# Three pairs in the seven products of SwiGLU's last down projection, and the norm's squares added on GpSimd

## The chip, the cores and the metric

The kernel runs on one core of a Trainium2 chip. The metric is the device time of one execution in microseconds (us). TensorE (PE in the profile) multiplies matrices, VectorE (DVE) and ScalarE (ACT) do elementwise work, GpSimd (POOL) does elementwise work and issues some DMAs, SyncE (SP) issues the other DMAs. A matmul result lands in a bank of PSUM; everything else lives in SBUF.

## What is computed

A trunk of two layers over a prompt of 512 tokens and a sample of 256, all in fp32. Each layer has a SwiGLU, a mixer (two kinds) and a second SwiGLU; a norm stands ahead of each and at the end.

```python
def swiglu(h, wg, wu, wd):
    return (jax.nn.silu(h @ wg) * (h @ wu)) @ wd      # 1024 -> 2816 -> 1024
def rmsnorm(x, g):
    return x * lax.rsqrt(jnp.mean(x * x, axis=-1, keepdims=True) + EPS) * g
def even_layer(x, ...):
    x = x + 0.5 * swiglu(rmsnorm(x, f1_n), f1_g, f1_u, f1_d)
    x = x + mixer_ab(rmsnorm(x, mix_n), ...)
    x = x + 0.5 * swiglu(rmsnorm(x, f2_n), f2_g, f2_u, f2_d)
def odd_layer(x, ...):      # the same with mixer_c, neighbourhood attention
```

## The kernel before, in words

The 768 tokens are the free dimension, in two halves of 384 (`HALVES`); the 1024 channels of x are eight tiles `x[0..7]` of 128 partitions. Each fp32 product is made of three single-pass matmuls by `mm3`: operands are split into a high part and the rest, and hi*hi, lo*hi and hi*lo are summed in PSUM. A weight tile of 128x512 is split by `wsplit`: ScalarE casts `whi`, VectorE subtracts for `wlo` (both in rings of five tiles, so that splits can run some way ahead of TensorE).

A SwiGLU goes by 11 pairs of 256 hidden channels (`NPAIR`). Its down projection is worked off for two pairs at a time by a 2x2 scheme of seven products in place of eight (Strassen and Winograd): the products are named by their data operand, b11, b21, t1, t2, t3, n4 and b22, and need sums of weight blocks (`sums`: s1 to s4, on VectorE or by accumulating DMAs) and of data blocks (`combine`). `down_last` does the last pairs and adds to x. Before, it takes pairs 8 and 9 through the seven products, 24 matmuls each, and pair 10 as a plain product (`plain`), 96 matmuls, with its own split weights (`lasts`) and operands (`operand`). The four calls are: layer 0's first SwiGLU, followed by the first mixer ("m0"); its second, followed by a SwiGLU ("f"); layer 1's first, followed by the second mixer ("m1"); its second, followed by the final norm ("last"). In "f" and "last" the order of the products is such that half 0 is done well ahead of half 1 (`lag`).

When a tile of x has its last addition, `final` calls `norm_add`: ScalarE squares it (`sq`), and VectorE adds the square to `acc` (L281). Once all eight tiles of a half are in, TensorE multiplies `ones` with `acc` (a sum over channels), ScalarE moves it to a small tile `sm`, GpSimd raises it to the power -1/2 (`sm<-sm,minus`, L321), and TensorE transposes the result (`ident,sm`). Ahead of a mixer, `final` also multiplies x by the gain and splits it (`xh` on ScalarE L992, `xl` on VectorE L993). The second mixer begins on GpSimd with ten additions of a mask `mb` and a bias (`add<-mb,ba` and `add<-mb,bb`, L1531); `mb` is cast in two pieces by VectorE from a loaded tile `mf`, whose buffer the second load shares.

TensorE's order is written by hand, by the order in which the code issues matmuls and by delays for the norms (`DELAY0`, `DELAYM` and others); the orders of the other engines come from a scheduler.

## Time and profile before

| what | value |
|---|---|
| median of three runs | 2553.0 us (2552.46 to 2553.01) |
| the profiled execution's own time | 2551.25 us |
| its span, from the first to the last instruction | 2549.5 us |
| mean granted TensorE clock | 0.999 |
| TensorE busy | 2532.9 us |
| VectorE busy | 2092.9 us |
| ScalarE busy | 1368.9 us |
| GpSimd busy | 323.5 us |

All times of single instructions are from that one execution. In lists of instructions the columns are start, duration, engine, line, operation, output<-inputs, shapes, and "xN" for N in a row; a bracket at the end gives the idle time of the engine before it and what ended it. Groups give busy time and mean nanoseconds. Rows of waits read: who waited for whom, us in total, times, longest.

### The profile page before, as it was taken

The numbers are of one execution on the slowest core, as the hardware profiler recorded it, in microseconds if no ns is written. First come the engines' busy times: TensorE is split into PE (matmuls) and PEld (weight loads), VectorE is DVE, ScalarE is ACT, GpSimd is POOL, SyncE is SP. The second block draws the span as 40 slices with busy tenths as digits, with TensorE's granted clock in tenths as the row PEclk, the third lists the DMA queues.
The fourth block names the chain that finished last, engine by engine and source line by source line (L and its number), as shares of the span: only waits on it lengthen the run. The fifth ranks groups of instructions, "written<-read, shape, count | busy, mean of one in ns | idle before, by whom it ended". The sixth has DMA issues, their size and how long they took to land.

```text
span 2549.5 us, 42554 instructions
## 1 busy us (share of the span) xinstructions
PE 2532.9 (99%) x15160; PEld 2459.3 (96%) x15160; DVE 2092.9 (82%) x4199; ACT 1368.9 (54%) x2843; POOL 323.5 (13%) x398
## 2 busy tenths in 40 slices
PE   9999999999999999999999999999999999999998
PEld 9999999988899999999999999998999899999998
DVE  8987888888879778888988888886667598878887
ACT  7544455546665545445655445554555475444553
POOL 1110111000111111110111011102112111101100
PEclk9999999999999999999999999999999999999999
DMA  8654555432256455552665455432222256545441
GB/s 238 159 133 119 132 134 147 146 94 64 77 142 175 117 128 127 131 130 80 156 150 135 119 128 125 120 127 69 65 61 78 76 150 166 131 121 125 124 125 53
DMA packets 187156, 310.88 MB, mean 122 GB/s; under 512 B 31680, under 2 KB 46528, under 8 KB 186944
## 3 DMA queue, kind: packets, MB, share of 16 engines
q1 hardware_dynamic: 149248, 240.49, 29.5%
q0 software_dynamic: 36864, 67.13, 16.9%
q8 instruction: 119, 1.95, 0.3%
q14 instruction: 93, 0.76, 0.1%
q10 hardware_dynamic: 832, 0.55, 0.1%
HBM read 298.65 MB, written 15.07 MB: 123 GB/s over the span
## 4 chain that ended last, share of the span: by engine, by line
PE 92%; DVE 4%; ACT 1%; issue 1%; DMA 1%; POOL 0%; ACTq 0%; DVEq 0%; SPq 0%; POOLq 0%
PE ps_mm L191 60%; PE ps_aux L191 30%; PE ps_aux L202 1%; DVE wlo L168 1%; DMA x<-in_x 0%; DMA s<-in_w 0%; DMA raw<-in_w 0%; DVE u L587 0%; DVE s L745 0%; DVE tl L255 0%; ACT p L1209 0%; ACT whi L167 0%; ACT ug L1484 0%; DVE o L1393 0%; DVE db L255 0%
## 5 line engine op out<-in xcount | busy, mean ns | idle before, releaser
L167 ACT CAST whi<-s 128x512 fp32r<-128x512 f32 x508 | 310.6, 621 | 384.5 <-PE ps_mm L191 199.0
L168 DVE TENSOR_TENSOR wlo<-s,whi 128x512 fp32r<-128x512 f32 x508 | 345.0, 687 | 173.6 <-ACT whi L167 152.1
L148 POOL DMA_DIRECT2D s<-in_w x256 | 224.0, 912 | 1440.0 <-DVE db L255 376.2
L167 ACT CAST whi<-rawp 128x512 fp32r<-128x512 f32 x344 | 211.5, 619 | 255.1 <-issue 100.0
L168 DVE TENSOR_TENSOR wlo<-rawp,whi 128x512 fp32r<-128x512 f32 x344 | 234.1, 685 | 23.2 <-ACT whi L167 14.2
L191 PE MATMUL ps_mm<-db,whi 128*128 128x384 f32 (+1 forms) x948 | 240.2, 334 | 0.0
L191 PE MATMUL ps_aux<-dt,whi 128*128 128x384 f32 x880 | 223.3, 334 | 0.0
L191 PEld LDWEIGHTS ps_mm<-db,whi 128*128 128x128 f32 x948 | 170.8, 188 | 0.0
L191 PE MATMUL ps_mm<-db,wlo 128*128 128x384 f32 (+1 forms) x474 | 158.3, 334 | 0.8 <-DVE wlo L168 0.8
L191 PEld LDWEIGHTS ps_aux<-dt,whi 128*128 128x128 f32 x880 | 158.9, 188 | 0.0
L191 PE MATMUL ps_aux<-dt,wlo 128*128 128x384 f32 x440 | 147.2, 335 | 0.4 <-DVE wlo L168 0.3
L167 ACT CAST whi<-raw 128x512 fp32r<-128x512 f32 x164 | 100.3, 619 | 68.6 <-PE ps_mm L191 44.6
L168 DVE TENSOR_TENSOR wlo<-raw,whi 128x512 fp32r<-128x512 f32 x146 | 98.9, 686 | 21.3 <-ACT whi L167 20.4
L587 DVE TENSOR_TENSOR u<-ps_aux,u 128x384 f32<-128x384 f32 x176 | 97.1, 552 | 7.7 <-PE ps_aux L191 7.7
L1209 ACT ACTIVATE p<-p,st 128x256 f32<-128x256 f32 (+3 forms) x144 | 69.1, 481 | 50.5 <-DVE st L1204 50.4
L191 PEld LDWEIGHTS ps_mm<-db,wlo 128*128 128x128 f32 x474 | 89.0, 188 | 1.4 <-DVE wlo L168 1.4
L581 ACT COPY u<-ps_mm 128x384 f32<-128x384 f32 x176 | 83.4, 474 | 1.9 <-PE ps_mm L191 1.6
L191 PEld LDWEIGHTS ps_aux<-dt,wlo 128*128 128x128 f32 x440 | 82.6, 188 | 1.0 <-DVE wlo L168 1.0
L745 DVE TENSOR_TENSOR s<-s,rawp 128x512 f32<-128x512 f32 x120 | 81.9, 687 | 2.0
L597 ACT ACTIVATE u<-u 128x384 f32<-128x384 f32 x88 | 46.2, 525 | 67.2 <-DVE u L596 67.1
L745 DVE TENSOR_TENSOR s<-rawp,s 128x512 f32<-128x512 f32 x120 | 81.9, 682 | 0.1
L191 PE MATMUL ps_aux<-dn,whi 128*128 128x384 f32 x320 | 81.2, 334 | 0.0
(772 smaller groups left out, 8228.7 us busy)
## 6 DMA issues: line engine op xcount, KB each, us to landing
rawp<-in_w SPq DMA_DIRECT2D x384, 256.0 KB, 3.2
s<-in_w SPq DMA_DIRECT2D x256, 256.0 KB, 2.8
s<-in_w POOLq DMA_DIRECT2D x256, 256.0 KB, 4.9
raw<-in_w SPq DMA_DIRECT2D x163, 256.0 KB, 2.9
xdm<-x SPq DMA_DIRECT2D x16, 384.0 KB, 2.3
x<-in_x SPq DMA_DIRECT2D x16, 192.0 KB, 4.6
x<-xdm SPq DMA_DIRECT2D x8, 384.0 KB, 4.9
tab<-skew SPq DMA_DIRECT2D x8, 256.0 KB, 4.0
```

What stands on the lines that cost most here:

```text
L148: self.nc.gpsimd.dma_start(f, y, accum_op=ALU.add)
L167: i = nc.scalar.copy(hi, src).ins
L168: self.behind = i, (eng or nc.gpsimd).tensor_tensor(out=lo, in0=src, in1=hi.bitcast(F32), op=ALU.subtract).ins
L191: self.nc.tensor.matmul(out, lhsT=lhsT, rhs=rhs, start=start, stop=stop, **kw)
L202: self.nc.tensor.transpose(out, src, self.ident)
L581: nc.scalar.copy(e[n, out], bank[key, n])
L587: nc.vector.tensor_tensor(out=t, in0=bank[key, n], in1=t, op=ALU.add)
L597: nc.scalar.activation(t, t, AF.Silu, scale=-1.0 if i else 1.0)
L745: f = lambda o, x, y: self.nc.vector.tensor_tensor(out=o, in0=x, in1=y, op=ALU.add)
L1209: nc.scalar.activation(outs[i - n0], outs[i - n0], AF.Exp, scale=-1.0, bias=mn[:, i : i + 1], accum_out=sm[:, i : i + 1])
```

## The change

`down_last` takes all three last pairs through the seven products, 36 matmuls each. A product works off pair 8 for its four banks, then pairs 9 and 10 bank by bank, so that banks are finished one after the other; the product that finishes half 1 in "f" (b22) and the last one in "m0" and "m1" (n4) take all three pairs bank by bank (`once`), and in "last" `ending` does the same with the narrow column slices. The code for the plain pair goes (`plain`, `lasts`, `operand`, `quads`, and `wsplit`'s kept and negated forms). In the three downs that are not followed by the end, `norm_add` puts the addition of squares on GpSimd (`aside`), and `final` calls `norm_add` after the gain and split of x, not ahead of them.

```diff
-            self.summed = i, nc.vector.tensor_tensor(out=self.acc[:, a:b], in0=self.acc[:, a:b], in1=sq, op=ALU.add).ins
+            eng = nc.gpsimd if self.aside else nc.vector
+            self.summed = i, eng.tensor_tensor(out=self.acc[:, a:b], in0=self.acc[:, a:b], in1=sq, op=ALU.add).ins
...
-        self.down_last(pre, range(NPAIR - 3, NPAIR - 1), d, hs[NPAIR - 1])
+        self.down_last(pre, range(NPAIR - 3, NPAIR), d, operands(NPAIR - 1))
...
-            t = s[n, "s2"] = self.fw.tile([P, 4, P], F32, tag="s", name=name, bufs=8)
+            t = s[n, "s2"] = a11 if n == NPAIR - 1 else self.fw.tile([P, 4, P], F32, tag="s", name=name, bufs=8)
...
+        def part(st, p, b, key, j, start, cols=slice(0, H)):
+            self.mm3(
+                bank[key, j][:, cols], (st[0][:, j, :], st[1][:, j, :]), [t[:, cols] for t in d[p][b]],
+                start and p == pairs[0], p == pairs[-1], not start,
+            )
+
+        def product(w, b, key, start, then, once=False):
+            for ps in (pairs,) if once else (pairs[:1], pairs[1:]):
+                st = {p: self.wsplit(w[p], nc.vector) for p in ps}
+                for j in range(4):
+                    for p in ps:
+                        if start and p == pairs[0]:
+                            bank[key, j] = self.psum()[:, :H]
+                        part(st[p], p, b, key, j, start)
+                    if ps[-1] == pairs[-1]:
+                        then(j)
...
+        def seed(j):
+            bank["Y", j] = self.psum(self.aux, "aux")[:, :H]
+            nc.scalar.copy(bank["Y", j], bank["X", j])
+
+        def below(j):
+            out(4 + j, 0, "Y")
             if not lag:
+                self.final(4 + j, H, T)
+
+        def ending():
+            st = {p: self.wsplit(s4[p], nc.vector) for p in pairs}
+            for js, cuts in ((0, 1), ((0, H),)), ((2, 3), CUTS):
                 for a, b in cuts:
                     for j in js:
+                        for p in pairs:
+                            part(st[p], p, "b22", "Z", j, False, slice(a, b))
+                        out(j, 1, "Z", a, b, j == 3)
                     if cuts is CUTS:
                         self.spawn(self.finish(1, H + a, H + b))
 
+        self.aside = not ends
+        more(own, 4)
+        product(w["a11"], "b11", "X", True, seed)
+        more(own, 2)
+        s2 = sums("s2")
+        product(w["a12"], "b21", "X", False, lambda j: out(j, 0, "X"))
+        more(self.later, 3)
+        product(s2, "t2", "Y", False, lambda j: add(j, 1, bank["Y", j]))
+        more(own, 5)
+        s4 = sums("s4")
+        fifth = sums("s1"), "t1", "Z", True, lambda j: add(4 + j, 1, bank["Z", j])
+        seventh = sums("s3"), "t3", "Y", False, lambda j: add(4 + j, 1, bank["Y", j])
+        third = s4, "b22", "Z", False, lambda j: out(j, 1, "Z")
+        fourth = w["a22"], "n4", "Y", False, lambda j: out(4 + j, 0, "Y")
         if lag:
+            product(*seventh)
+            product(*fourth)
             self.half_done(0)
+            product(*fifth[:4], lambda j: out(4 + j, 1, "Z"))
+            if ends:
+                ending()
+            else:
+                product(*third, True)
                 self.half_done(1)
         else:
+            product(*fifth)
+            product(*third)
+            product(*seventh)
+            product(*fourth[:4], below, True)
+        self.aside = False
...
-        self.norm_add(m, c0, c1)
         if self.nxt[0] in ("m0", "m1") and c1 == T:
 
             gain = self.gain(m)
...
                 nc.vector.scalar_tensor_tensor(
                     out=lo, in0=src, scalar=gain, in1=hi.bitcast(F32), op0=ALU.mult, op1=ALU.subtract
                 )
+        self.norm_add(m, c0, c1)
```

**GpSimd before the second mixer.** Between layer 1's first down projection and its mixer, GpSimd had before the last `MEMSET` of the mixer's tiles, four additions of mask and bias, the norm's power, and the other additions:

```order
L1548 MEMSET p_19650 128x96
L1531 TENSOR_TENSOR add<-mb,ba 128x192
L1531 TENSOR_TENSOR add<-mb,ba 128x256
L1531 TENSOR_TENSOR add<-mb,ba 128x192
L1531 TENSOR_TENSOR add<-mb,ba 128x256
L321 TENSOR_TENSOR sm<-sm,minus 128x6
L1531 TENSOR_TENSOR add<-mb,ba 128x192
L1531 TENSOR_TENSOR add<-mb,bb 128x160 x2
L1531 TENSOR_TENSOR add<-mb,ba 128x192
L1531 TENSOR_TENSOR add<-mb,bb 128x160 x2
```

Now the squares' additions come first (twelve of them stand ahead of these rows), and all ten additions of mask and bias stand ahead of the power:

```order
L1490 MEMSET p_19676 128x96
L274 TENSOR_TENSOR acc<-acc,sq 128x384 x2
L1473 TENSOR_TENSOR add<-mb,ba 128x192
L1473 TENSOR_TENSOR add<-mb,ba 128x256
L1473 TENSOR_TENSOR add<-mb,ba 128x192
L1473 TENSOR_TENSOR add<-mb,ba 128x256
L1473 TENSOR_TENSOR add<-mb,ba 128x192
L1473 TENSOR_TENSOR add<-mb,bb 128x160 x2
L1473 TENSOR_TENSOR add<-mb,ba 128x192
L1473 TENSOR_TENSOR add<-mb,bb 128x160 x2
L314 TENSOR_TENSOR sm<-sm,minus 128x6
L1473 TENSOR_TENSOR add<-mb,ba 128x192 x2
```

The power has moved behind six further additions, and behind the last squares. Before the first mixer, GpSimd had nothing between its last DMA and the power; now fourteen `acc<-acc,sq` stand there.

**VectorE at the end of the first down projection.** Names: `x` is a tile of x, `xl` the split for the mixer, `wlo<-raw` the mixer's weights. Before:

```order
L879 TENSOR_TENSOR x_107<-x_107,ps_aux_5262 128x384
L879 TENSOR_TENSOR x_107<-x_107,ps_mm_5594 128x384
L168 TENSOR_TENSOR wlo_5789<-raw_5781,whi_5788 128x512
L281 TENSOR_TENSOR acc<-acc,sq 128x384 x2
L993 SCALAR_TENSOR_TENSOR xl_5180<-x_107,gains,xh_5179 128x512
L993 SCALAR_TENSOR_TENSOR xl_5180<-x_107,gains,xh_5179 128x256
L879 TENSOR_TENSOR x_108<-x_108,ps_aux_5271 128x384
L879 TENSOR_TENSOR x_108<-x_108,ps_mm_5596 128x384
L168 TENSOR_TENSOR wlo_5798<-raw_5792,whi_5797 128x512
L281 TENSOR_TENSOR acc<-acc,sq 128x384 x2
```

Now:

```order
L861 TENSOR_TENSOR x_106<-x_106,ps_aux_5294 128x384
L934 SCALAR_TENSOR_TENSOR xl4a<-x_105,gains,xh4a 128x512
L160 TENSOR_TENSOR wlo_5791<-raw_5785,whi_5790 128x512
L934 SCALAR_TENSOR_TENSOR xl5a<-x_106,gains,xh5a 128x512
L861 TENSOR_TENSOR x_107<-x_107,ps_aux_5302 128x384
L861 TENSOR_TENSOR x_108<-x_108,ps_aux_5310 128x384
L160 TENSOR_TENSOR wlo_5795<-raw_5787,whi_5794 128x512
L160 TENSOR_TENSOR wlo_5804<-raw_5798,whi_5803 128x512
L934 SCALAR_TENSOR_TENSOR xl_5180<-x_107,gains,xh_5179 128x512
```

The additions of squares are gone from here; where a tile got its two additions, its squares and its splits in one go, the tiles now alternate, since the banks of the last product are finished one after the other and the 256-column splits of each tile stand ahead of its last addition.

**TensorE at the very end.** `khi` and `klo` are pair 10's split weights, `ones,acc` and `ones,sq` the sums of the squares, `ident,sm` the transposes. Before:

```order
L191 MATMUL ps_mm_29244<-db_29063,khi_29327 128x128
L191 MATMUL ps_mm_29244<-db_29062,klo_29328 128x128
L191 MATMUL ps_aux_29416<-ones,acc 128x1
L191 MATMUL ps_aux_29416<-ones,sq 128x1
L191 MATMUL ps_aux_29416<-ones,acc 128x1
L191 MATMUL ps_aux_29416<-ones,sq 128x1
L191 MATMUL ps_mm_29244<-dh,khi_29071 128x128 x2
L191 MATMUL ps_mm_29244<-dh,klo_29072 128x128
L191 MATMUL ps_mm_29244<-dh,khi_29075 128x128 x2
L191 MATMUL ps_mm_29244<-dh,klo_29076 128x128
L202 MATMUL ps_aux_29433<-ident,sm 128x128 x2
L191 MATMUL ps_aux_29455<-ones,acc 128x1
```

Now:

```order
L183 MATMUL ps_mm_29285<-db_29142,whi_29367 128x128
L183 MATMUL ps_mm_29285<-db_29141,wlo_29368 128x128
L183 MATMUL ps_aux_29456<-ones,acc 128x1
L183 MATMUL ps_aux_29456<-ones,sq 128x1
L183 MATMUL ps_aux_29456<-ones,acc 128x1
L183 MATMUL ps_aux_29456<-ones,sq 128x1
L183 MATMUL ps_aux_29467<-ones,acc 128x1
L183 MATMUL ps_aux_29467<-ones,sq 128x1
L194 MATMUL ps_aux_29473<-ident,sm 128x128 x2
L194 MATMUL ps_aux_29495<-ident,sm 128x128
```

All sums of squares now stand behind the last product's matmuls, where before those of the 256 columns stood ahead of its last six.

More of the change, by code (lines that the diff above doesn't have):

```diff
@@ L855, in part @@
[L855 to L872 removed]
+                next(gen, None)
@@ L887, in out @@
                 self.final(m, half * H + a, half * H + b)
-        def seed(to, key, j):
-            bank[to, j] = (self.psum(self.aux, "aux") if to == "Y" else self.psum())[:, :H]
-            nc.scalar.copy(bank[to, j], bank[key, j])
-        def lasts(i):
-            return [self.wsplit(quads_last[2 * i + k], nc.vector, lag and i == 0, -1 if i else 1) for k in (0, 1)]
-        s2 = sums("s2")
-        st = split(w["a11"])
-        s3 = sums("s3")
-        for j in range(4):
-            part(st, "b11", "X", j, True)
-            seed("Y", "X", j)
@@ L902, in down_last @@
-        quads_last = quads(last)
-        st = split(s2)
-        for j in range(4):
-            part(st, "t2", "Y", j, False)
-            add(j, 1, bank["Y", j])
-        s4 = sums("s4")
-        st = split(w["a12"])
-        for j in range(4):
-            part(st, "b21", "X", j, False)
-        operand(0, 0)
-        operand(1, 0)
-        def seventh():
-            st = split(s3) if lag else {p: s3[p, "split"] for p in pairs}
-            for j in range(4):
-                part(st, "t3", "Y", j, False)
-                if lag:
-                    add(4 + j, 1, bank["Y", j])
@@ L921, in fifth @@
-        def fifth():
-            st = split(sums("s1"))
-            for j in range(4):
-                part(st, "t1", "Z", j, True)
-                add(4 + j, 1, bank["Z", j])
-        def third(u):
-            st = {p: self.wsplit(s4[p], nc.vector, lag and p == pairs[1]) for p in pairs}
+        def seed(j):
[3 more added lines that the diff above has]
+            out(4 + j, 0, "Y")
             if not lag:
-                s3.update({(p, "split"): self.wsplit(s3[p], nc.vector, p == pairs[1]) for p in pairs})
-            ends = self.following[0] == "last"
-            for js, cuts in (((0, 1), ((0, H),)), ((2, 3), CUTS)) if ends else ((range(4), ((0, H),)),):
+                self.final(4 + j, H, T)
@@ L980, in final @@
+        self.aside = False
     def final(self, m, c0, c1):
```

85 lines of the change are left out of this document (7 added, 78 removed).

## The prediction

> **What bounds the kernel now.** I read the page first: busy times, the chain of work that ended last, the granted clock.
>
> ```profile
> PE 2532.9 (99%) x15160; PEld 2459.3 (96%) x15160; DVE 2092.9 (82%) x4199; ACT 1368.9 (54%) x2843; POOL 323.5 (13%) x398
> PE 92%; DVE 4%; ACT 1%; issue 1%; DMA 1%; POOL 0%; ACTq 0%; DVEq 0%; SPq 0%; POOLq 0%
> ```
>
> TensorE is busy 99% of the 2549.5 us span and carries 92% of the chain. Fewer matmuls are therefore time, unless another engine then comes late. The waits of TensorE, and busy times by stretches of 10 us, say how near the others are:
>
> ```profile
> PE ps_mm L191 <- DVE wlo L168: 2.3, 7, 0.4
> PE ps_aux L202 <- POOL sm L321: 2.1, 1, 2.1
> ...
> 480.00:490.00 10.00, 10.00 (x57) 9.56 (x57) 9.45 (x18) 8.09 (x18) 0.00 (x0) 1.00 0.59 197
> 490.00:500.00 10.00, 10.00 (x58) 9.68 (x57) 9.52 (x20) 7.60 (x16) 0.00 (x0) 1.00 0.64 217
> 1170.00:1180.00 10.00, 10.00 (x60) 10.00 (x59) 9.90 (x20) 5.32 (x10) 0.00 (x0) 1.00 0.25 80
> ```
>
> The columns are total, PE, PEld, DVE, ACT, POOL, clock, DMA share, GB/s. At the ends of the down projections (480 to 500 us before the first mixer, 1170 to 1180 before the second layer's first SwiGLU) VectorE has 0.1 to 0.55 us free in ten, GpSimd computes nothing, and TensorE hardly waits. The margin is thin there, and the change rearranges exactly these stretches.
>
> **Fewer matmuls.** Pair 10 took 96 mm3 parts outside the seven products; as a third pair it takes 84. In the three downs that another stage follows that is 12 matmuls of 384 columns fewer each; in the last it is 6 of 384, 6 of 256 and 6 of 128. Their price is from a stretch of 384-column work and two rows of the tail:
>
> ```profile
> 200.00:300.00 100.00, 100.00 (x579) 100.00 (x578) 80.62 (x145) 48.14 (x94) 12.19 (x14) 1.00 0.53 127
> ...
> 2539.53 0.42 PE L191 MATMUL ps_mm<-dh,khi 128*128 128x128 f32 x2
> 2539.90 0.39 PE L191 MATMUL ps_mm<-dh,khi 128*128 128x128 f32 x2
> ```
>
> 100/579 is 0.173 us each at 384 columns; from 2539.53 to 2539.90 run three of 128, 0.12 each. Those of 256 lie between; I take 0.12 (0.173 would add 0.3). Saved: 12 x 0.173 = 2.1 us in each of three downs (6.3), and 6 x 0.173 + 12 x 0.12 = 2.5 in the last: 8.8 us if all of it reaches the end.
>
> **What the squares' adds cost on GpSimd.** 42 adds `acc<-acc,sq` of 128x384 leave VectorE, 14 in each of those three downs. No such add runs on GpSimd before; its neighbours do:
>
> ```profile
> L1030 POOL TENSOR_TENSOR y<-x,acc 128x256 f32<-128x256 f32 x2 | 1.4, 724 | 1.0 <-ACT acc L1017 1.0
> L1030 POOL TENSOR_TENSOR y<-x,acc 128x128 f32<-128x128 f32 x2 | 0.9, 458 | 0.9 <-ACT acc L1017 0.9
> L168 POOL TENSOR_TENSOR wlo<-raw,whi 128x512 fp32r<-128x512 f32 x18 | 24.2, 1350 | 169.8 <-ACT whi L167 147.5 <-DMA raw<-in_w 16.4 <-PE ps_mm L191 5.8
> ```
>
> 128 more columns cost 0.724 - 0.458 = 0.27 us, so 384 columns are about 0.99 us (estimate; the 512-column row says at most 1.35). Whether the two run beside each other is shown where GpSimd splits weights in the first mixer:
>
> ```profile
> 652.01 0.68 DVE L255 TENSOR_TENSOR ol2a<-o,oh2a 128x512 fp32r<-128x512 f32 x1
> 652.06 1.79 POOL L168 TENSOR_TENSOR wlo<-raw,whi 128x512 fp32r<-128x512 f32 x1 [8.26 <-ACT whi L167]
> 652.61 1.78 DVE L255 TENSOR_TENSOR ol4a<-o,oh4a 128x512 fp32r<-128x512 f32 x1
> ...
> 689.10 1.30 POOL L168 TENSOR_TENSOR wlo<-raw,whi 128x512 fp32r<-128x512 f32 x1 [8.56 <-ACT whi L167]
> 689.77 0.64 DVE L1147 TENSOR_TENSOR x<-ps_mm,xold 128x256 f32<-128x256 f32 x1
> ```
>
> GpSimd's split, 1.30 alone, takes 1.79 where VectorE's ol2a stands across its start; then VectorE's ol4a, 0.68 alone, lasts until 0.54 after GpSimd is through (652.06 + 1.79 = 653.85; 652.61 + 1.78 = 654.39). With one operand in PSUM (689.77) VectorE finishes within GpSimd's 1.30. So I take operations with two SBUF operands on the two engines to run one after the other: VectorE's wlo and xl do, its adds from PSUM don't. The Trainium skill, "SBUF — State Buffer", section "Who interferes with whom", states this as a rule: a VectorE instruction with two SBUF inputs contends with a GpSimd one that reads SBUF, and the loser "fully blocks"; these rows agree. By that rule the sums below stand; without it the adds would only relieve VectorE and the no-lock rival below would be the sum.
>
> **End of the first down (before the first mixer).** From the first bank of the product that closes half 1 to the norm's matmuls, the changed order has on TensorE 90 matmuls of 384 and 21 of 512 columns.
>
> ```profile
> 498.34 0.40 PE L191 MATMUL ps_mm<-xh0a,whi 128*128 128x512 f32 x1
> 503.24 1.39 PE L191 MATMUL ps_aux<-ones,acc 128*128 128x1 f32 x12
> ...
> 491.00 0.75 DVE L993 SCALAR_TENSOR_TENSOR xl4a<-x,gains,xh4a 128x512 fp32r<-128x512 f32 x1
> 491.67 0.48 DVE L993 SCALAR_TENSOR_TENSOR xl4b<-x,gains,xh4b 128x256 fp32r<-128x256 f32 x1
> 492.07 0.55 DVE L879 TENSOR_TENSOR x<-x,ps_aux 128x384 f32<-128x384 f32 x1
> 492.53 0.55 DVE L879 TENSOR_TENSOR x<-x,ps_mm 128x384 f32<-128x384 f32 x1
> ...
> 500.56 1.02 DVE L281 TENSOR_TENSOR acc<-acc,sq 128x384 f32<-128x384 f32 x2
> 502.56 1.28 DVE L168 TENSOR_TENSOR wlo<-raw,whi 128x512 fp32r<-128x512 f32 x2
> ```
>
> The 21 took 503.24 - 498.34 = 4.9 us, so TensorE needs 90 x 0.173 + 4.9 = 20.5 us. The two-SBUF work in that stretch: 7 xl of 512 at 0.67 (491.00 to 491.67), 8 of 256 at 0.40, 6 wlo at 0.64 = 11.7 us on VectorE, and 11 adds x 0.99 = 10.9 on GpSimd: 22.6 us one after the other. The first add starts some 1.5 us in (x, then its square). So the last add comes at least 22.6 - 20.5 = 2.1 us late; at most 22.6 + 1.5 + 12 PSUM adds x 0.46 (none beside GpSimd) - 20.5 = 9.1. I take 5.5, about the middle, since both engines work in a fixed order and can't always find a partner that fits. Before, the last add ended at 501.6, 1.7 before its use at 503.24; that cover is gone. Net: 5.5 - 2.1 = **+3.4** (bounds 0 and +7.0).
>
> **End of the third down (before the second mixer).** The stretch has the same 90 matmuls and 27 of 512 columns: 15.6 + 27 x 0.233 = 21.9 us.
>
> ```profile
> 1710.24 1.27 DVE L993 SCALAR_TENSOR_TENSOR xl<-x,gains,xh 128x448 fp32r<-128x448 f32 x3
> 1714.17 1.00 ACT L1105 COPY accp<-acc 128x448 f32<-128x448 f32 x3
> ```
>
> VectorE's xl come in three pieces per tile (about 1.2 us a tile), with 5 wlo 12.2 us; GpSimd 10.9; a copy of the sums on ACT follows, 1.2 with its start: 24.3 against 21.9, so 2.4 late at least, 9.4 with the same extras, 6 taken. Behind it stands a second price:
>
> ```profile
> 1715.09 0.41 DVE L1518 CAST mb<-mf 128x512 bf16<-128x512 f32 x1
> 1715.65 3.75 POOL L1531 TENSOR_TENSOR add<-mb,ba 128x192 f32<-128x192 bf16 x4 [52.65 <-DVE mb L1518]
> 1716.73 1.39 PE L191 MATMUL ps_aux<-ones,accp 128*128 128x1 f32 x12
> 1718.88 0.77 DVE L1518 CAST mb<-mf 128x448 bf16<-128x448 f32 x1 [2.17 <-DMA mf<-in_nmask]
> 1719.36 1.50 POOL L321 TENSOR_TENSOR sm<-sm,minus 128x6 f32<-128x6 f32 x1
> 1720.84 0.64 POOL L1531 TENSOR_TENSOR add<-mb,ba 128x192 f32<-128x192 bf16 x1
> 1720.91 0.87 PE L202 MATMUL ps_aux<-ident,sm 128*128 128x128 f32 x6
> 1723.15 1.12 POOL L1531 TENSOR_TENSOR add<-mb,bb 128x160 f32<-128x160 bf16 x2
> ```
>
> GpSimd's power `sm<-sm,minus` ends at 1720.86 and TensorE's transposes of it start at 1720.91: no slack. In the changed order the six bias adds that ran after it (1720.84 to 1724.27, 3.4 us) stand ahead of it, and they need the second cast of the mask, 4.6 us after the first begins (1715.09 to 1719.65). From the last square's add T: the power ends at about T + 4.6 + 3.4 + 1.5 = T + 9.5 if the first cast begins with T; the transposes are wanted at T + 1.2 + (1720.91 - 1716.73) = T + 5.4. That is 4.1 late; with the cast a little before T, 3 taken, 1 at least. Net: 6 + 3 - 2.1 = **+6.9** (bounds +1.3 and +11.4).
>
> **The second down** is followed by a SwiGLU, whose norm of half 1 is wanted much later. Its adds fall where VectorE is 9.0 to 9.9 of 10 busy; 0.99 less the 0.5 that VectorE gets back (500.56, two in 1.02) loses 0.5 per add, 2 us if the four adds of one product were not covered by the ring of five split weight tiles, 0 if they are. I take 0.6: **-1.5** (bounds -2.1 and 0; +2 if two products fail).
>
> **The last down** keeps its adds on VectorE.
>
> ```profile
> 2538.67 0.33 PE L191 MATMUL ps_aux<-ones,acc 128*128 128x1 f32 x2
> 2540.02 0.70 POOL L321 TENSOR_TENSOR sm<-sm,minus 128x2 f32<-128x2 f32 x1 [15.19 <-ACT sm L301]
> 2540.12 0.28 PE L191 MATMUL ps_mm<-dh,klo 128*128 128x128 f32 x1
> 2540.77 0.43 PE L202 MATMUL ps_aux<-ident,sm 128*128 128x128 f32 x2 [0.37 <-DVE x L877]
> ```
>
> The norm of the 256-column slice started 1.7 us before the last matmul's end (2540.40); now its `ones` rows stand behind all matmuls, at 2540.4 - 2.5 = 2537.9 instead of 2538.67. The tail of scaling and stores hangs on that: **-0.8** (bounds -2.5 and 0).
>
> ACT (54% busy) loses eight copies and gains splits; SP gains four loads net, GpSimd eight accumulating ones ahead of its adds, issued long before their use: nothing.
>
> **The sum**: 3.4 - 1.5 + 6.9 - 0.8 = +8.0 on the profiled 2551.25 us, 2559.3. That execution lies 1.75 below the median of the runs, so I add the 8.0 to 2553.0: 2561. By the bounds 2549.7 to 2571 or 2573.
>
> **Rivals.** *No lock* (0.25): VectorE's own load falls to 11.7 + 12 x 0.46 = 17.2 of 20.5 us in the first stretch, the adds are early, and only the power's new place costs: -2.1, -2.1, +1.5 (4.1 late, 0.5 less for a cast that comes a little earlier, less 2.1), -0.8: -3.5, 2549.5, within 0.2% (5.1 us, what a measurement here can tell from no change). For it: in the before rows no add of a square meets GpSimd; against: the rows at 652 us. *Saving kept, power covered* (0.15, the other side): the place is GpSimd's row order before the second mixer, the price 3.4. If the mask's casts come early enough (the first at or before 1710, 5 us earlier, and adds done by T + 4) the power isn't late, and with the lead of five split tiles holding in all downs the sum is -8.8 to -6.3: 2544 to 2547. Against: the first cast stands behind nearly every xl in VectorE's order. *Lock* (0.60) is the forecast, own range 2550 to 2573; I put 0.52 of it above +0.2% and 0.08 within.
>
> Faster: 0.15 and 0.04 of no lock, 0.19. Same: 0.08 + 0.21 = 0.29. Slower: 0.52. The range reaches to the no-lock case and into the kept saving: 2547 to 2573.
>
> **What the changed profile would show.** Right: GpSimd adds near 0.99 us or stretched by VectorE's, and wlo and xl of over 1 us beside them; waits of TensorE for wlo and for the sums before both mixers; `sm<-sm,minus` at the second mixer behind ten bias adds, with a wait of some 3 us at the transposes. Wrong: wlo and xl at their usual 0.68 and 0.75 beside the adds; no wait for `ones`; or adds far from 0.99.

## The result, and the profile after

The changed kernel takes 2573.8 us, the kernel before 2552.7 (medians of six runs each): a ratio of 1.0085, with an interval of 1.0075 to 1.0096. That is 21 us slower, where 8 were forecast, and 0.8 us above the upper end of the range. The profiled execution of the changed kernel took 2574.48 us, its span is 2571.7.

The busy times on its page:

```profile
PE 2536.4 (99%) x15106; PEld 2457.0 (96%) x15106; DVE 2119.9 (82%) x4193; ACT 1375.0 (53%) x2855; POOL 379.9 (15%) x448
```

TensorE runs 54 instructions fewer than before and is nevertheless busy 3.5 us longer, so instructions got longer. VectorE has six instructions fewer and is busy 27 us longer, and that is two things. The third pair brings it 36 instructions more and 20.6 us (4235 and 2113.5 us with the additions back on VectorE, in the first experiment, against 4199 and 2092.9 before). Then 42 additions go, and it is busy 6.4 us longer all the same: there, too, instructions got longer.

To place the loss, both traces are cut where the SwiGLUs are undisturbed: at the start of the 11th, 31st, 51st and 76th multiplication `u<-u,acc` of VectorE, one in each of the four SwiGLUs (two lines of the kernel have that name; the first of them counts, 22 times in each). Between two cuts lies the end of one down projection and what follows it. Busy times by stretch, total first, then PE, PEld, DVE, ACT, POOL, clock, DMA share, GB/s; before:

```profile
238.68:907.43 668.75, 665.74 (x3944) 631.99 (x3943) 564.62 (x1191) 376.05 (x765) 66.80 (x71) 1.00 0.46 123
907.43:1362.83 455.40, 455.40 (x2634) 455.10 (x2634) 386.38 (x709) 242.35 (x482) 54.63 (x62) 1.00 0.51 129
1362.83:2223.79 860.96, 859.39 (x5414) 825.94 (x5413) 672.26 (x1439) 455.03 (x1003) 131.24 (x176) 1.00 0.42 110
```

and after:

```profile
239.76:913.56 673.80, 667.01 (x3932) 630.73 (x3931) 572.16 (x1188) 376.50 (x765) 85.30 (x87) 1.00 0.46 123
913.56:1375.79 462.23, 455.00 (x2622) 452.79 (x2622) 394.64 (x702) 244.88 (x488) 73.11 (x78) 1.00 0.51 129
1375.79:2242.87 867.08, 860.75 (x5402) 826.39 (x5401) 678.64 (x1435) 455.41 (x1003) 149.14 (x193) 1.00 0.41 110
```

The differences of the totals are the loss by stage; total less PE is TensorE's idle time. What is left of the spans (2549.5 and 2571.7) lies before the first cut (1.1 us; experiments with that code unchanged gave -0.5 to +1.6) and behind the last one.

| stage | shift, us | TensorE idle, before and after | forecast |
|---|---|---|---|
| first down, first mixer | +5.05 | 3.01, 6.79 | +3.4 |
| second down, SwiGLU | +6.83 | 0.00, 7.23 | -1.5 |
| third down, second mixer | +6.12 | 1.57, 6.33 | +6.9 |
| last down, end | +3.12 | | -0.8 |

The second down alone holds 8.3 of the 14.2 us by which these two executions miss the forecast (22.2 us between the spans, 8.0 forecast). The waits of TensorE, where before only 0.4 us stood at most for any `wlo`:

```profile
PE ps_mm L183 <- DVE wlo L160: 5.6, 8, 2.4
PE ps_aux L183 <- DVE wlo L160: 4.2, 7, 1.9
PE ps_mm L183 <- DVE x L859: 3.6, 2, 2.1
PE ps_mm L183 <- ACT p L612: 1.5, 1, 1.5
PE ps_mm L183 <- DVE xl L934: 1.4, 1, 1.4
PE ps_aux L183 <- POOL acc L274: 0.6, 1, 0.6
```

GpSimd's additions themselves, as a group (busy time and mean ns of one behind the bar):

```profile
L274 POOL TENSOR_TENSOR acc<-acc,sq 128x384 f32<-128x384 f32 x42 | 51.8, 1241 | 138.6 <-ACT sq L269 116.4 <-PE ps_mm L183 21.6
```

**At the end of the first down**, in order of time, VectorE and GpSimd, then TensorE:

```profile
497.90 2.50 POOL L274 TENSOR_TENSOR acc<-acc,sq 128x384 f32<-128x384 f32 x2 [0.35 <-ACT sq L269]
498.03 1.50 DVE L160 TENSOR_TENSOR wlo<-raw,whi 128x512 fp32r<-128x512 f32 x1
499.46 1.49 DVE L934 SCALAR_TENSOR_TENSOR xl5a<-x,gains,xh5a 128x512 fp32r<-128x512 f32 x1
502.17 5.40 POOL L274 TENSOR_TENSOR acc<-acc,sq 128x384 f32<-128x384 f32 x4 [1.77 <-ACT sq L269]
503.83 1.48 DVE L934 SCALAR_TENSOR_TENSOR xl<-x,gains,xh 128x512 fp32r<-128x512 f32 x1
505.37 0.50 PE L183 MATMUL ps_mm<-xl,whi 128*128 128x512 f32 x1 [1.41 <-DVE xl L934]
507.63 0.83 PE L183 MATMUL ps_aux<-ones,acc 128*128 128x1 f32 x6 [0.57 <-POOL acc L274]
```

While GpSimd adds, VectorE's `wlo` and `xl` take 1.5 us where they took 0.64 to 0.75, and the additions take 1.25 to 1.35. The last one ends at 507.57 (before: 501.58). TensorE waits for `xl`, then for the sums.

**In the second down** and the SwiGLU behind it:

```profile
1201.30 0.68 DVE L738 TENSOR_TENSOR s<-rawp,s 128x512 f32<-128x512 f32 x1
1203.77 0.67 DVE L738 TENSOR_TENSOR rawp<-rawp,rawp 128x512 f32<-128x512 f32 x1
1204.84 0.67 DVE L160 TENSOR_TENSOR wlo<-s,whi 128x512 fp32r<-128x512 f32 x1
1205.57 0.45 PE L183 MATMUL ps_aux<-dt,wlo 128*128 128x384 f32 x1 [1.86 <-DVE wlo L160]
...
1233.04 1.98 DVE L372 TENSOR_TENSOR tmp<-x 128x384 f32<-128x384 f32 x1
1234.68 1.79 POOL L274 TENSOR_TENSOR acc<-acc,sq 128x384 f32<-128x384 f32 x1
1234.94 0.55 DVE L859 TENSOR_TENSOR x<-ps_mm,x 128x384 f32<-128x384 f32 x1
1235.41 1.50 DVE L397 SCALAR_TENSOR_TENSOR tmp<-tmp,gains 128x384 f32<-128x384 f32 x1
1237.56 0.44 PE L183 MATMUL ps_mm<-b110h,wlo 128*128 128x384 f32 x1 [1.32 <-DVE wlo L160]
```

There are two causes. Weight sums of a later product (`s`, `rawp`, L738) stand on VectorE ahead of the `wlo` that TensorE needs at 1205. And from 1227 on the next SwiGLU prepares its data on VectorE (`tmp`, two operands in SBUF) beside GpSimd's additions: 1.98 and 1.50 us each. The `x` at 1234.94 reads PSUM and takes its usual 0.55 inside GpSimd's 1.79.

**At the end of the third down**, TensorE, GpSimd and a busy table as above:

```profile
1726.76 0.50 PE L183 MATMUL ps_mm<-xh0a,wlo 128*128 128x512 f32 x1 [2.42 <-DVE wlo L160]
1731.24 4.52 POOL L1473 TENSOR_TENSOR add<-mb,ba 128x192 f32<-128x192 bf16 x5
1738.52 1.35 POOL L314 TENSOR_TENSOR sm<-sm,minus 128x6 f32<-128x6 f32 x1
1739.93 0.87 PE L194 MATMUL ps_aux<-ident,sm 128*128 128x128 f32 x6 [1.45 <-POOL sm L314]
```

```profile
1726.00:1732.00 6.00, 5.24 (x16) 4.16 (x17) 6.00 (x8) 2.53 (x7) 6.00 (x16) 0.72 0.66 201
```

The power `sm<-sm,minus` stands behind all ten bias additions and TensorE waits 1.45 us for it. The larger wait is for the mixer's first `wlo`, and behind it the granted clock is 0.72 over six us: 6 x 0.28 = 1.7 us of TensorE's work lost, without any wait to show for it. The same, 1.71 us, is lost behind the waits at 505 to 508 us.

**In the last down**, VectorE, then TensorE:

```profile
2549.45 2.18 DVE L318 SCALAR_TENSOR_TENSOR y<-x,gains,ps_aux 128x384 f32<-128x384 f32 x4
2554.01 1.13 DVE L318 SCALAR_TENSOR_TENSOR y<-x,gains,ps_aux 128x384 f32<-128x384 f32 x2
2555.52 1.21 DVE L859 TENSOR_TENSOR x<-ps_mm,x 128x384 f32<-128x384 f32 x3
2556.46 0.44 PE L183 MATMUL ps_mm<-db,whi 128*128 128x128 f32 x2 [2.05 <-DVE x L859]
2556.84 0.63 PE L183 MATMUL ps_mm<-db,whi 128*128 128x128 f32 x2
```

The scalings `y` of half 0, which no matmul waits for, stand ahead of the additions to x that release the narrow matmuls. TensorE stands 2.05 us, and from 2556.9 on two matmuls of 128 columns take 0.63 instead of 0.39: half the clock to the end. (Whether the clock falls behind this wait differs from one execution to the next, see the filled gap below.)

### The profile page after: what moved, and what is told of

Same layout as the page of the kernel before. It is cut to its first block, busy times and chain, and to the rows that moved or that the text cites. A ratio compares the mean times of both kernels' runs of the same rounds, so it can differ in the third digit from the quotient of the medians.

```text
span 2571.7 us, 42536 instructions
## 1 busy us (share of the span) xinstructions
PE 2536.4 (99%) x15106; PEld 2457.0 (96%) x15106; DVE 2119.9 (82%) x4193; ACT 1375.0 (53%) x2855; POOL 379.9 (15%) x448
## 4 chain that ended last, share of the span: by engine, by line
PE 49%; DVE 3%; POOL 0%; ACT 0%; issue 0%; DMA 0%; DVEq 0%; SPq 0%; ACTq 0%; POOLq 0%
PE ps_mm L183 32%; PE ps_aux L183 16%; PE ps_aux L194 1%; DVE wlo L160 1%; DVE y L318 0%; POOL add L1473 0%; DVE tmp L397 0%; DVE x L861 0%; ACT whi L159 0%; DVE tmp L372 0%; DVE x L859 0%; DMA raw<-in_w 0%; DVE s L738 0%; ACT sq L269 0%; DMA s<-in_w 0%
## 5 line engine op out<-in xcount | busy, mean ns | idle before, releaser
L160 DVE TENSOR_TENSOR wlo<-s,whi 128x512 fp32r<-128x512 f32 x520 | 353.4, 687 | 175.5 <-ACT whi L159 159.3
L149 POOL DMA_DIRECT2D s<-in_w x264 | 232.1, 907 | 1458.2 <-DVE wlo L160 380.6
L183 PE MATMUL ps_mm<-db,whi 128*128 128x384 f32 (+1 forms) x1068 | 270.8, 334 | 2.1 <-DVE x L859 2.1
L183 PE MATMUL ps_aux<-dt,whi 128*128 128x384 f32 x960 | 243.6, 334 | 0.0
L183 PEld LDWEIGHTS ps_mm<-db,whi 128*128 128x128 f32 x1068 | 193.2, 189 | 2.5 <-DVE x L859 2.3
L183 PE MATMUL ps_mm<-db,wlo 128*128 128x384 f32 (+2 forms) x534 | 178.5, 334 | 0.0
L183 PEld LDWEIGHTS ps_aux<-dt,whi 128*128 128x128 f32 x960 | 173.3, 188 | 0.0
L183 PE MATMUL ps_aux<-dt,wlo 128*128 128x384 f32 x480 | 160.7, 335 | 2.2 <-DVE wlo L160 2.1
L183 PEld LDWEIGHTS ps_mm<-db,wlo 128*128 128x128 f32 x534 | 101.0, 189 | 0.0
L183 PE MATMUL ps_aux<-dn,whi 128*128 128x384 f32 x352 | 90.7, 338 | 0.7 <-DVE x L861 0.7
L738 DVE TENSOR_TENSOR s<-s,rawp 128x512 f32<-128x512 f32 x120 | 81.8, 687 | 2.0
L738 DVE TENSOR_TENSOR s<-rawp,s 128x512 f32<-128x512 f32 x120 | 82.6, 688 | 0.1
```

Source lines behind the costliest of these rows:

```text
L149: self.nc.gpsimd.dma_start(f, y, accum_op=ALU.add)
L160: self.behind = i, (eng or nc.gpsimd).tensor_tensor(out=lo, in0=src, in1=hi.bitcast(F32), op=ALU.subtract).ins
L183: self.nc.tensor.matmul(out, lhsT=lhsT, rhs=rhs, start=start, stop=stop, **kw)
L738: f = lambda o, x, y: self.nc.vector.tensor_tensor(out=o, in0=x, in1=y, op=ALU.add)
```

## The experiments

Shifts below are against the kernel before, by the same cuts, from one profiled execution each; ratios are over all runs, with their interval. Kernels start from the changed one unless said otherwise.

A single stage is not sure to a microsecond, since stretches of half clock fall differently from one execution to the next. The kernel with the filled gap has the changed kernel's code up to the last down, and still stands at 7.7, 8.4 and 6.0 where the changed kernel has 5.05, 6.83 and 6.12: its half clock costs 5.1, 1.7 and 1.7 us in these stages, the changed kernel's 1.7, 0 and 3.4. Kernels whose last down is the changed kernel's range there from 0.8 to 3.1.

| kernel | first | second | third | last | median us | ratio |
|---|---|---|---|---|---|---|
| changed kernel | 5.05 | 6.83 | 6.12 | 3.12 | 2573.8 | 1.0085 (1.0075 to 1.0096) |
| adds on VectorE | 0.2 | 2.0 | 8.4 | 1.3 | 2565.3 | 1.0048 (1.0033 to 1.0063) |
| before, adds on GpSimd | 0.6 | 4.1 | 5.7 | 0.05 | 2563.6 | 1.0045 (1.0029 to 1.0062) |
| power first | 5.3 | 6.9 | 4.5 | 1.9 | 2572.5 | 1.0077 (1.0062 to 1.0092) |
| filled gap | 7.7 | 8.4 | 6.0 | 0.75 | 2571.4 | 1.0075 (1.0060 to 1.0090) |
| adds on VectorE, not by bank | 5.8 | 4.1 | 8.4 | 1.5 | 2570.7 | 1.0072 (1.0057 to 1.0087) |
| weights first | 1.6 | 1.9 | 3.8 | 0.8 | 2559.5 | 1.0030 (1.0018 to 1.0042) |
| weights first, not by bank | 6.7 | 2.6 | 0.9 | 1.5 | 2565.8 | 1.0053 (1.0036 to 1.0070) |
| orders mended | 3.6 | 0.3 | 2.2 | -0.7 | 2555.2 | 1.0010 (1.0001 to 1.0019) |
| norm later | 0.2 | 0.3 | 0.2 | -1.1 | 2552.3 | 1.0001 (0.9992 to 1.0010) |
| norm later still | 0.25 | 0.27 | 0.34 | -1.0 | 2552.3 | 0.9999 (0.9991 to 1.0008) |
| orders mended, adds on GpSimd | 7.4 | 6.6 | 8.1 | -0.7 | 2572.8 | 1.0080 (1.0065 to 1.0095) |

**The adds back on VectorE.**

```diff
-        self.aside = not ends
+        self.aside = False
```

> The changed kernel with the additions of squares left on VectorE in all four downs; the three-pair products, the order of the norm after the splits and the power's place behind ten bias adds stay. Stage shifts against the kernel before were, in the changed kernel, +1.1 us up to the first SwiGLU's gates, +5.1 over the end of the first down and the first mixer, +6.8 over the second down, +6.1 over the third, +3.1 over the last. Theory L (operations with two SBUF operands on VectorE and GpSimd run one after the other, and that makes TensorE wait): the second down falls from +6.8 to between -2 and +1, the first from +5.1 to between -2 and +2, the third from +6.1 to +1 to +4 (the power's place remains), the last stays at +3; in all 2556 to 2562 us. Rival C (three pairs in seven products leave less VectorE time and less cover by themselves; the adds' engine hardly matters): VectorE gets 0.47 us more per add, the stages stay within 1.5 us of the changed kernel's or get slower; 2571 to 2578 us.

Measured: 2565.3 us, above the 2556 to 2562 expected and below the rival's 2571 to 2578. The first two downs give back 4.9 us each; the third, for which +1 to +4 was expected, gets worse, +8.4. The last falls by 1.8 though nothing in it was changed: it has the same idle time and less half clock. Its page, and the mixer's start on VectorE and TensorE:

```profile
PE 2529.1 (99%) x15106; PEld 2453.6 (96%) x15106; DVE 2113.5 (83%) x4235; ACT 1374.5 (54%) x2855; POOL 331.9 (13%) x406
```

```profile
1717.97 2.36 DVE L160 TENSOR_TENSOR wlo<-raw,whi 128x512 fp32r<-128x512 f32 x2
1719.16 0.80 PE L183 MATMUL ps_mm<-xh0a,wlo 128*128 128x512 f32 x1 [7.60 <-DVE wlo L160]
```

VectorE has 42 instructions more and is busy 6.4 us less: beside GpSimd's additions its other work had grown by more than all 42 additions cost it. In the third down the order of VectorE is a new problem: the first `wlo` of the mixer stands behind every `xl` and every addition, TensorE waits 7.60 us, and 5.1 us more go to the half clock that follows.

**The adds alone, in the kernel before.**

```diff
+            eng = nc.gpsimd if self.aside else nc.vector
+            self.summed = i, eng.tensor_tensor(out=self.acc[:, a:b], in0=self.acc[:, a:b], in1=sq, op=ALU.add).ins
...
+        self.aside = kind != "last"
         self.down_last(pre, range(NPAIR - 3, NPAIR - 1), d, hs[NPAIR - 1])
+        self.aside = False
```

> The kernel before with one part of the change alone: the additions of squares in the three downs that another stage follows run on GpSimd (42 of 128x384); pair 10 stays a plain product and the norm stays ahead of the splits. Theory L: the adds last 1.0 to 1.3 us, VectorE's operations with two SBUF operands beside them 1.2 to 1.5 instead of 0.55 to 0.75, and each of the three downs ends 2 to 6 us later: 2559 to 2570 us. Rival C: VectorE is relieved of 42 x 0.47 us, nothing gets later: 2550 to 2554 us.

Measured: 2563.6, 11.8 us over the kernel before as it was measured with it (2551.9), with all of its matmuls still there and its own order of products:

```profile
L283 POOL TENSOR_TENSOR acc<-acc,sq 128x384 f32<-128x384 f32 x42 | 47.4, 1133 | 152.6 <-ACT sq L278 113.6 <-PE ps_mm L192 38.4
```

So the additions cost by themselves; the first down there keeps a cover (+0.6).

**The power ahead of the bias additions.**

```diff
         self.ry = self.norm_tok(acc, 0, T)
+        if cols:
+            with self.tc.issue_after(self.powered):
+                self.first_bias()
...
-        adds[0], adds[1] = bias(0), bias(1)
+        self.first_bias = lambda: adds.update({0: bias(0), 1: bias(1)})
```

> The changed kernel with one edit: the ten first additions of mask and bias of the second mixer are issued behind the norm's power on GpSimd instead of ahead of it. If the power's place costs what the prediction said, the transposes no longer wait for it (1.45 us of waiting in the changed kernel) and the third down falls from +6.1 to +4 to +5; the bias adds, 7 us, then end some 7 us after the power, before the first scores need them. If the ones are late anyway, or the bias adds become the wait, the third down stays at +6 or grows. Whole: 2571 to 2573 us by the first, 2574 or more by the second.

Measured: the wait for `sm` is gone and the third down falls from +6.1 to +4.5, 1.6 us; TensorE's idle time there falls by 1.4, and the half clock is the same 3.4 us. The mechanism is as forecast, at half its price of 3. Over all runs the difference from the changed kernel (1.0077 against 1.0085) is within the intervals; the stage shows it, the total does not.

**A gap filled.** Eight matmuls of 512 columns that compute nothing wanted stand in the last down ahead of the narrow slices.

```diff
                 for a, b in cuts:
+                    if a:
+                        self.warm(8)
                     for j in js:
```

> The changed kernel with eight matmuls of 512 columns on constant operands (their result is used by nothing) put into the last down between the 256-column and the 128-column slices, where TensorE idled 2.1 us (2554.3 to 2556.5) and the granted clock then read 0.5 until the end. Theory G (idling brings the half clock): the clock reads 1.0 through the 128-column matmuls, a group of three takes 0.36 instead of 0.64 us, six groups and the sums of squares end 2 to 2.5 us earlier, and the last stage falls from +3.1 to about +1: 2571 to 2572 us. Rival (the clock falls for another reason, or VectorE's scaling sets the end anyway): the clock still reads 0.5 or the end stays within 0.5 us of the changed kernel's.

```profile
2557.61 1.99 PE L190 MATMUL ps_aux<-onesr 128*128 128x512 f32 x8
2559.83 0.44 PE L183 MATMUL ps_mm<-db,whi 128*128 128x128 f32 x2 [0.23 <-DVE x L859]
2560.22 0.39 PE L183 MATMUL ps_mm<-db,whi 128*128 128x128 f32 x2
```

Measured: 2571.4 us; the interval overlaps the changed kernel's. With the gap filled, two narrow matmuls take 0.39 again, and the last stage falls from +3.1 to +0.75, though the narrow matmuls start no earlier (2559.83 is 3.4 later than 2556.46, all of which stems from the stages before). But a gap that is not filled can leave the clock alone too. In "the mixer's first weights ahead", below, the last down is the changed kernel's:

```profile
2544.28 0.44 PE L183 MATMUL ps_mm<-db,whi 128*128 128x128 f32 x2 [2.06 <-DVE x L859]
2544.67 0.39 PE L183 MATMUL ps_mm<-db,whi 128*128 128x128 f32 x2
```

The wait is the same, the matmuls behind it run at full clock, and the stage stands at +0.8. So of the +3.1 in the changed kernel's profile some 2 us are the half clock, as the rows show; that filling the gap took them away is not shown by this one execution, since chance does it as well.

**Gaps of made length.** In the kernel before, 16 gaps: a matmul whose operand comes from a chain of k copies on ScalarE.

```diff
+        self.nc.tensor.matmul(ps[:, :P], lhsT=self.onesr, rhs=self.onesr, start=True, stop=True)
+            self.nc.scalar.copy(t, ps[:, :P])
+            for _ in range(k):
+                self.nc.scalar.copy(t, t.bitcast(F32))
+        self.nc.tensor.matmul(ps[:, :P], lhsT=self.onesr, rhs=t, start=True, stop=True)
```

> The kernel before with sixteen made gaps, one at the start of each two-pair down projection (four in each SwiGLU): TensorE waits for a chain of 1 to 13 copies of 128x128 on ScalarE, about 0.2 to 0.3 us each, whose result goes nowhere. Theory G (a gap of some length halves the granted clock for a fixed time): gaps under about 1.9 us leave the clock at 1.0; gaps over 2.1 us bring 0.5 for about 3.4 us each (1.7 us lost on top of the gap); between the two it depends on where the gap falls. Rival (only a gap of 3.4 us or more counts, or the fall comes from something else in those stages): gaps of 2.1 to 3.3 us leave the clock at 1.0 here.

Two gaps on TensorE, and busy times and clock over the ten us around each:

```profile
850.46 0.33 PE L205 MATMUL ps_aux<-idle,onesr 128*128 128x128 f32 x1 [1.96 <-ACT idle L203]
2200.23 0.33 PE L205 MATMUL ps_aux<-idle,onesr 128*128 128x128 f32 x1 [2.28 <-ACT idle L203]
```

```profile
845.00:855.00 10.00, 8.04 (x47) 7.84 (x47) 5.44 (x10) 5.85 (x15) 1.79 (x2) 1.00 0.67 158
2196.00:2206.00 10.00, 7.72 (x36) 7.51 (x36) 3.65 (x8) 5.28 (x14) 1.79 (x2) 0.83 0.56 114
```

The kernel took 2627.3 us (one run). All gaps from 0.68 to 1.96 us (4) left the clock at 1.00; all from 2.28 to 3.56 (8) cost 1.71 us of work, as 3.41 us at half clock; 3.88, 4.21 and 5.20 cost 3.42, and 4.54 cost 1.7. One more such stretch, at 675 us, has no made gap ahead of it, only a wait of 1.44 us that every kernel here has; 10 of the 14 traces have that wait without a dip.

So the length of a wait alone does not decide. The next kernel waits 2.29 us at 1240.9 and the clock stays at 1.00; the wait of 1.86 us in the second down leaves it at 1.00 in the changed kernel and halves it in the one with the filled gap (1208.9). What fits all 14 traces is a grid. Counted from the clock's first rise, every stretch of half clock begins and ends at a whole multiple of 3.413 us, to about a thousandth of a step; in the changed kernel the dips begin at steps 147, 501, 504 and 747, before at 743. And the columns of the matmuls that start in one step tell what the next one gets. Of the steps at full clock all 43 with fewer than 2560 columns were followed by half clock, none of the 10,304 with more than 4224, and 9 of the 56 from 2560 to 4224. A step full of 512-column matmuls, 0.23 us each, holds some 7600. A wait of 2 us can therefore cost nothing where a line of the grid cuts it, and 1.7 us more where one step holds it whole. This is read from the traces; no run moved the grid.

**Not bank by bank.** The adds on VectorE, and no product by bank.

```diff
-            for ps in (pairs,) if once else (pairs[:1], pairs[1:]):
+            for ps in (pairs[:1], pairs[1:]):
```

> The changed kernel with the adds on VectorE and the last product (n4 before the mixers, b22 before the SwiGLU) worked off as the others: pair 8 for four banks, then pairs 9 and 10 bank by bank. TensorE then needs one split weight tile for its first 2.1 us in place of three in 1.6 us, so its waits for wlo at the start of that product (1.1 us in the first down, 1.5 in the third) should fall to 0.5 or less; against that the four banks end within 3.1 us at the product's end in place of 4.7, and VectorE's work on them bunches up there. If the split tiles are the tighter of the two, the first down falls from +0.2 to about -1; if the bunching is, it rises to +2 or more. Second down within 1 us of +2.0 (its long wait lies at t3, which isn't changed). Whole: 2560 to 2568 us.

Measured: 2570.7, above the 2560 to 2568 expected and slower by 5.4 than with the banks one after the other; the first down goes from +0.2 to +5.8. All tiles of x then end together, and TensorE waits 6.4 us for the mixer's first `wlo`. The second down, which was to stay at +2.0, has +4.1, 1.7 of it half clock. With the weights of the mixer in this order on VectorE the products by bank are a gain of the change, not a cost.

**The mixer's first weights ahead.** The adds on VectorE, the power first, and the second mixer's first weights with high priority in the scheduler.

```diff
-            ws = self.unit("l1_w_qkv", 0, KD, pr * P, P), self.unit("l1_w_qkv", 0, KD, 1024 + pr * P, P)
+            with nullcontext() if pr else self.tc.high_priority():
+                ws = self.unit("l1_w_qkv", 0, KD, pr * P, P), self.unit("l1_w_qkv", 0, KD, 1024 + pr * P, P)
```

> The changed kernel with the adds on VectorE, the power ahead of the bias adds, and the second mixer's first weights split ahead of the last splits of x on VectorE. With the adds on VectorE alone the third down stood at +8.4: TensorE waited 7.6 us for the mixer's first wlo, which stood behind every xl and every add of squares, and then ran 10 us at half clock. Theory O (VectorE's order of the mixer's weights sets this): that wait falls below 2 us, the clock stays at 1.0, and the third down falls from +8.4 to between 0 and +3. Rival (the work itself is too much for VectorE): the wait moves to xl or to the sums, and the stage stays over +5. First and second down as with the adds on VectorE: +0.2 and +2.0. Whole: 2555 to 2560 us by the first.

Measured: 2559.5, as expected; the third down falls from +8.4 to +3.8, where at most +3 was expected. The 7.60 us wait is gone, shorter ones (1.5 for `wlo`, 1.2 for `xl`) stay, and with them 3.4 us of half clock: the order was half of the answer.

**Both.** The same, without the banks one after the other.

> Both edits: adds on VectorE, power ahead of the bias adds, second mixer's weights split first, and the last product not bank by bank. If both theories hold, the first down is near -1, the third between -1 and +2, the second and the last as before this edit (+2.0 and +1 to +3): 2552 to 2557 us. If the bunching at the end costs more than the split tiles, it is slower than the same kernel with the last product bank by bank.

Measured: 2565.8. The first down, whose weights were not moved, is again 5 us worse; the third is better than by bank (+0.9 against +3.8) in this execution, but only by the half clock, 0 against 3.4 us; TensorE idles 0.4 us longer. So where the mixer's weights come first, the two forms are about equal but for the clock. The first down with its weights first and not by bank was not run. For the sum as it stands, by bank is better.

**The orders mended.** Beside the above, in "f" and "last" the weight sums s4 are issued behind n4, the last down's final additions to x and the first mixer's first weights have high priority.

```diff
-        s4 = sums("s4")
+        s4 = None if lag else sums("s4")
...
             self.half_done(0)
+            s4 = sums("s4")
+            third = s4, *third[1:]
...
-                        out(j, 1, "Z", a, b, j == 3)
+                        with self.tc.high_priority():
+                            out(j, 1, "Z", a, b, j == 3)
...
-        wk = self.unit("l0_w_in", 0, KD, 1536, P)
-        wv = self.unit("l0_w_in", 0, KD, 1664, P)
+        with self.tc.high_priority():
+            wk = self.unit("l0_w_in", 0, KD, 1536, P)
+            wv = self.unit("l0_w_in", 0, KD, 1664, P)
```

> The changed kernel with the adds on VectorE, the power first, both mixers' first weights split ahead of the last splits of x, and two more edits of order: in the second and the last down the sums s4 (three operations of VectorE that only b22 needs) come behind n4 instead of ahead of t3, and the last down's final additions to x go ahead of the scaling of half 0 on VectorE. If each wait of TensorE came from VectorE's order: the 2.0 us wait for wlo at t3 goes, the second down falls from +1.9 to about 0; the 2.1 us wait in the last down falls below 1 us, the clock stays at 1.0 to the last matmul, the last stage falls from +0.8 to +1.5 down to between -2 and -1; the first down loses its waits of 1.2 and 1.1 us for wlo and falls from +0.2 to between -2 and -1; the third stays near +3.8 or lower. Whole: 2549 to 2554 us, within 0.2% of the kernel before. If VectorE's work itself is too much in these stretches, the waits only move to other operands and the whole stays over 2556.

Measured: 2555.2, between the two ranges expected. The second down falls to +0.3, the last to -0.7. The first was to fall to between -2 and -1 and has +3.6, of which 3.4 are clock; and one of its two waits for `wlo`, 1.1 us, stays. TensorE at the norm's sums, and the stretch behind it:

```profile
504.39 0.83 PE L183 MATMUL ps_aux<-ones,acc 128*128 128x1 f32 x6 [0.21 <-DVE acc L274]
505.91 1.42 PE L183 MATMUL ps_aux<-ones,acc 128*128 128x1 f32 x6 [0.70 <-DVE acc L274]
```

```profile
505.00:512.00 7.00, 6.30 (x19) 5.19 (x20) 2.93 (x7) 0.79 (x2) 1.35 (x1) 0.57 0.78 268
```

Two waits of 0.21 and 0.70 us around twelve matmuls of one column: 7 x 0.43 = 3.0 us lost here, 3.4 with the rest of the dip. The twelve take 2.3 us and bring twelve columns: the step of the grid from 502.56 to 505.98, which holds both waits, has 1543 columns, three matmuls of 512 and seven of one. That a matmul counts by its columns fits all the traces, but no run varied it alone.

**The norm later.** The same, with the mixer's norm later in TensorE's order, by the table that delays it.

```diff
-DELAYM = (3.5, 5.0)
+DELAYM = (4.5, 4.5)
```

> The kernel with the orders mended, and the norm's sums in both mixers put two groups of three 512-column matmuls later on TensorE, the transposes one group. In the profile of the mended kernel TensorE waited 0.3 us for xl and twice for the last squares around the sums (0.9 us in all), whose one-column matmuls take another 1.4 us; the clock then stood at 0.5 for 6.8 us (3.4 lost). If short waits and one-column matmuls add up to the idling that halves the clock, the sums now wait for nothing, the clock stays at 1.0 in the first mixer, the first down falls from +3.6 to about 0, the third from +2.2 to about +0.5: 2550 to 2553 us. If one-column matmuls alone bring it, the loss stays: 2554 to 2556.

```profile
PE 2526.1 (99%) x15106; PEld 2450.3 (96%) x15106; DVE 2111.6 (83%) x4235; ACT 1373.8 (54%) x2855; POOL 330.4 (13%) x406
```

> The same, with sums and transposes three groups later than in the mended kernel. As the one before if nothing waits for the transposes; if the mixers' first results wait for the scale that comes from them, the first and third down gain a wait of up to 2 us: 2551 to 2555 us.

Measured: 2552.3 both, with (4.5, 4.5) and with (5.5, 5.0); no different from the kernel before (1.0001 and 0.9999). The dips at 505 and 1724 us are gone. TensorE is busy 6.8 us less than before (2526.1 against 2532.9), and idle 6.3 us more (2549.0 - 2526.1 = 22.9 against 16.6): the saved matmuls are there, and waits of 0.3 to 1.5 us, for `wlo` and `xl` above all, have taken their place.

**The adds on GpSimd again, with the orders mended.** The kernel "orders mended", but for

```diff
-        self.aside = False
+        self.aside = not ends
```

> The kernel with the orders mended, with the additions of squares on GpSimd again in the three downs. Theory L: VectorE's xl and wlo beside them take 1.2 to 1.5 us, the sums and splits come late again, and the first three downs lose 3 to 5 us each against the mended kernel with the adds on VectorE: 2562 to 2570 us. If the adds hurt only through the orders, the kernel is within 2 us of the mended one or faster: 2551 to 2557 us.

```profile
L274 POOL TENSOR_TENSOR acc<-acc,sq 128x384 f32<-128x384 f32 x42 | 51.4, 1228 | 140.2 <-ACT sq L269 118.0 <-PE ps_mm L183 21.4
```

Measured: 2572.8, 17.6 us over the same kernel with the adds on VectorE and above the 2562 to 2570 expected; the last down, which has none on GpSimd in either, is the same to 0.1 us. That is nearly the whole loss of the change. Against "norm later" 21.6 us separate the two profiled spans. Half of them are clock: dips at 505, 662, 1717 and 1734 us, 10.2 us, where "norm later" has none ahead of its end. The one at 662, 1.7 us, differs by chance: it stands behind the wait of some 1.4 us that every kernel has there. Most of the rest are waits that name VectorE or GpSimd.

## Why the prediction was right and wrong

**The lock** was right, and is shown: one line that moves the additions is worth 8.5 us as the change stands (2573.8 to 2565.3, 1.0085 to 1.0048) and 17.6 with the orders mended, and the work that grew beside them has two operands in SBUF, while that with one in PSUM kept its time. *No lock* and *saving kept* both fell. The additions were priced at 0.99 us; the least took 1.005 (0.990 in the kernel before with the adds on GpSimd), the mean 1.24.

**The matmuls' price** held: 6.8 of 8.8 us show as less busy time in "norm later". The other 2 may be the first matmul behind each wait, which takes longer (0.50 us at 505.37 above against 0.40 at 498.34 in the prediction's rows, both of 512 columns); that is argued, not shown.

**The second down** is the step that failed: "I take 0.6", "2 us if the four adds of one product were not covered by the ring of five split weight tiles". Only TensorE's weights were counted there. But the down is followed by a SwiGLU whose data sums and splits are two-operand work on VectorE, and they fall right beside the additions (1.98 and 1.50 us each, 1233 to 1237). And the ring gives no lead where sums of another product stand ahead of the split in VectorE's order: moving s4, the one edit of "orders mended" that touches this down, took it from 1.9 to 0.3. Of the 8.3 us that this term was off, 4.9 are the additions (6.83 to 1.97), 1.7 the place of s4, and the rest, 1.8, is what even the mended form loses.

**The first down** had the right mechanism and a sum 1.65 us too small. Counted from the first cut, the norm's sums start 3.3 us later than before (507.63 - 503.24 - 1.08), where 3.4 were forecast. But only 0.57 us is a wait for the sums, where the forecast put the whole delay; 1.41 is a wait for `xl`, 1.3 are four shorter ones for `wlo`. The excess is the half clock behind them, 1.71 us, for which the prediction had no term.

**The third down** was right in its total (6.9 against 6.1) by luck, and wrong in its parts: no wait for the sums (6 taken), 1.45 for the power (3 taken), 2.4 for the mixer's first `wlo` and 1.1 for the last product's, and two dips of the clock, 3.4.

**The last down** was called -0.8 and came to +3.1. The prediction moved the `ones` matmuls forward and did not ask what stands ahead of the final additions on VectorE. Before, 16.8 us passed from the end of half 0's products to the first matmul of 128 columns (2519.89 to 2536.71), and the eight scalings of half 0 fitted in between. Now 24 matmuls fewer stand there, TensorE is through after 13.3 us (2541.09 to 2554.40), and the scalings collide with the additions that it then waits for. Some 2 us of the 3.1 are the half clock, of which other kernels with the same last down have less or nothing (+0.8 to +1.9). With those additions first it is -0.7, as forecast.

**The clock** is the term that was missing altogether: 1.7 us in the first stage, 3.4 in the third, and the longer matmuls at the end. The profile of before shows 1.00 everywhere up to the tail; its longest wait up to there is 1.41 us. The Trainium skill, "TensorE: Matmul & The Clock Gate", section "Part 1: The HAM clock gate (the 'warmup' mystery)", states that the clock drops to half after an idle window of about 3.4 us, and that the window runs freely. The half rate, the 3.41 us of one dip and the fixed grid agree with the traces here. Its section "HAM oscillation — how this bites in real kernels" asks for no idle gaps above some 3.4 us. Here made gaps of 2.28 us were already enough, and every step of the grid with fewer than 2560 columns, a third of a full one, was followed by half clock, so the measurement decides.

**What stays open:** why three pairs, with every order mended and no dip, only tie. The waits that eat the saving are named by engine (the two longest that the kernel before doesn't have, 1.1 and 1.5 us, are for the last product's `wlo`), but no run took them away.

## What to carry to other kernels

Before moving two-operand work to GpSimd, list all two-SBUF-operand work that VectorE has in the same stretch, the next stage's preparation included: the move pays only if that list is nearly empty. When a saving shortens TensorE's work by microseconds, read on every other engine what stands ahead of the instruction that TensorE will want next, since the saved time was the cover for that order. And count waits of TensorE as dearer than they look: where they add up to some 2 us within 3.4 us, 1.7 us of half clock can come on top, in one run and not in the next.
